# Attention layer of a hybrid backbone: rotated heads turned one block later, modulation vectors spread as two exact parts

## The chip, the cores and the metric

The kernel runs on one core of one Trainium2 chip. The time is the device time of one execution in microseconds, as the median of several runs. The engines are named as in the profile: PE (TensorE matmul; PEld its weight loads), DVE (VectorE), ACT (ScalarE), POOL (GpSimd) and SP (the queue that issues most of the DMAs).

## What is computed

Two layers over 256 latent tokens and 256 context tokens of width 1024. The first layer is attention, the second a state-space mixer; each is followed by a mixture of experts. The change lies in the first layer alone, up to its output projection. Cut to what matters:

```python
m  = split(silu(c) @ mod_w[layer] + mod_b[layer], 6)       # modulation of the latents
mc = split(silu(c_ctx) @ mod_w[layer] + mod_b[layer], 6)   # modulation of the context
xn = modulate(rms_norm(h, norm1_g), m[0], m[1])
hp = xn @ w_in                       # q and k of 8+2 heads, v, then q, k, v of 4 differential heads
qa, ka = rms_norm(qa, q_g), rms_norm(ka, k_g)
qa, ka, qb, kb = apply_rope(...)     # x * cos + rotated(x) * sin
p  = softmax(q @ k.T * scale)        # the differential heads: softmax(s1) - lam * softmax(s2)
h  = h + m[2] * (concat(p @ v) @ w_out)
h  = h + m[5] * hier_moe(modulate(rms_norm(h, norm2_g), m[3], m[4]))
```

A modulation vector is one row for all latent tokens and one for all context tokens. "Spreading" it means writing these two rows into all 128 partitions, 64 for each.

## The kernel before, in words

Latents and context are held together as four tiles of 128 rows (64 of the context, 64 latents). **Projection** (lines 474 to 572): the input weights come in five chunks (keys and values of the plain heads; their queries; queries of the differential heads; their keys; their values), and for each chunk there is a unit for each of the four row tiles. I call them blocks 0 to 19; block 4 is the first of the second chunk. Block `k` has a product `mm` and, if its chunk is rotated (blocks 0 to 15), a turn `tr`. `mm` is 8 x 3 matmuls into one PSUM bank (`mm3`, line 337: weights and activations are split in a high and a low part of type fp32r), then `rotate` (line 489), which is ACT's square (L495), a reduction, a reciprocal root in 12 tiny DVE operations (`rms`, line 282), a scaling (L500; these only in blocks 0 to 7) and the rotation itself (L505, L511 twice, L512), nearly all on DVE. `tr` (`head_pairs`, line 515) turns the rotated block on PE (L518), four transposes of 128 x 128 or one, and ACT copies it out (L530, L535 or L522).

The order is written out by hand with `pipeline` (line 189), which issues stage `n` of unit `k - lag[n]` in step `k`. With the lags (0, 2) the order on PE is mm(0), mm(1), mm(2), tr(0), mm(3), tr(1), mm(4), tr(2) and so on; the turn of a block waits for its L512.

The weights are split by `Splitter.half` (line 349): ACT rounds a quarter of a chunk to `whi` (L358), POOL computes `wlo` (L360). There are five buffers of each, so that of the next chunk only the first quarter is ready ahead; quarter 2 of a chunk takes the buffer that the last block of the chunk before gives up after its first six matmuls, and so on. Before block 12 the constants of the state-space layer are issued (`ssm_lambda`, line 1402): about a hundred small DVE operations, each in a fixed order behind the one before and behind block 11's rotation, and POOL copies of their results (L1508 to L1514).

**Attention** (lines 575 to 720): 48 head units (two query blocks, latents and context, four differential heads and eight plain ones each) with four stages at the lags (0, 3, 5, 10): scores and softmax, transposing the probabilities, the product with V, the last turn. Twelve more units are put in after every four or so of them, two for each of six modulation vectors (`mod_half`, line 229). Their first stage, `product`, is 8 matmuls of 1 MB of weights twice (L248) and an addition of the bias on DVE (L254) into the tile `mrow`; their second, `spread`, three units later, is one matmul of two rows picked by `sel2` (L258), and one copy or multiplication out of PSUM (L264, L266).

The compiler's scheduler sets each engine's final order by its own model from this order of issue; each engine then works its list in order. PSUM has six banks for all of this and two for the product with V. The tile pool `cx` holds eight score tiles `e`, two tiles `ob` and one `sq`.

```python
pipeline([unit(c, j) for c in range(5) for j in range(4)], (0, 2))          # line 572
t1 = (m5, H1[:, 0, :])[nrot[0] // 2 % 2][...]                               # line 503: four buffers
units.insert(10 * i + 5 * hf + 3, mod_half(*m[:3], hf, *m[3:]) + (None, None))  # line 718
pipeline(units, (0, 3, 5, 10))                                              # line 719
```

Of the kernel before, what the change touches and what calls it, by code (L numbers as in the profile page):

```python
# [10 lines left out]
F32 = mybir.dt.float32  # L11
# [3 lines left out]
FR = mybir.dt.float32r  # L15
AF = mybir.ActivationFunctionType
OP = mybir.AluOpType
# [113 lines left out]
def bc(ap, shape):  # L131
    return ap.to_broadcast(shape)
# [3 lines left out]
def hybrid(ctx: ExitStack, tc: tile.TileContext, A, out, taps=None, stop=None):  # L136
    nc = tc.nc
    taps = taps or {}
    V_ = nc.vector
# [29 lines left out]
    sm = ctx.enter_context(tc.tile_pool(name="sm", bufs=1))  # L169
# [3 lines left out]
    def bank(tag="b", name="bank"):  # L173
        return psp["p"].tile([128, 512], F32, tag=tag, bufs=psp[tag], name=name)
# [14 lines left out]
    def pipeline(units, lags):  # L189

        for k in range(len(units) + max(lags)):
            for n, lag in enumerate(lags):
                if 0 <= k - lag < len(units) and n < len(units[k - lag]) and units[k - lag][n]:
                    units[k - lag][n]()

    def wh(src, name, load=None):

        load = load or (lambda a: w8(a, name=name, shape=(4, 512)))
        hs = [load(src[:, 4 * i:4 * i + 4, :]) for i in range(2)]
        return lambda kk: hs[kk // 4][:, kk % 4, :]  # L200
# [8 lines left out]
    sel2 = cst[:, C_SEL2:C_SEL2 + 128]  # L209
# [16 lines left out]
    cp = [nc.scalar.copy, V_.tensor_copy]  # L226


    def mod_half(o, layer, sec, hf, sel, g=None, lean=False, room=None):


        n = 2 * sec + hf
        st = {}

        def product():
            w = wh(A["modw"][layer, n], "wmod", room and room[0])
            br = room[1] if room else brow
            sh = (lambda x: x) if len(br.shape) == 2 else (lambda x: x.rearrange("p (a b) -> p a b", b=128))
            nc.sync.dma_start(br[0:2], A["modb"][layer:layer + 1, n * 512:(n + 1) * 512].to_broadcast([2, 512])
                              if len(br.shape) == 2 else  # L240
                              sh(A["modb"][layer:layer + 1, n * 512:(n + 1) * 512]).to_broadcast([2, 4, 128]))
            if g is not None:
                st["gb"] = room[3] if room else sm.tile([128, 512], F32, tag="gb", bufs=1, name="gb")
                nc.sync.dma_start(st["gb"], g[:, hf * 512:(hf + 1) * 512].to_broadcast([128, 512]))
            pm = bank(name="pm")
            for kk in range(8):
                i = kk % 4
                nc.tensor.matmul(pm[32 * i:32 * i + 32, :], lhsT=cs[:, kk, :], rhs=w(kk), start=kk < 4, stop=kk >= 4)  # L248
            st["m"] = room[2] if room and room[2] is not None else sm.tile([128, 512], F32, tag="mrow", bufs=1, name="mrow")
            st["br"] = br  # L250
            if lean:
                nc.scalar.copy(st["m"], pm)
            else:
                V_.tensor_add(sh(st["m"]), sh(pm), br)  # L254

        def spread():
            pb = bank(name="pb")
            nc.tensor.matmul(pb, lhsT=sel, rhs=st["m"], start=True, stop=not lean)  # L258
            if lean:
                nc.tensor.matmul(pb if len(st["br"].shape) == 2 else pb.rearrange("p (a b) -> p a b", b=128), lhsT=sel,  # L260
                                 rhs=st["br"], start=False, stop=True)
            t = st["m"] if o is None else o[:, hf * 512:(hf + 1) * 512]
            if g is None:
                nc.scalar.copy(t, pb)  # L264
            else:
                V_.scalar_tensor_tensor(t, in0=pb, scalar=1.0, in1=st["gb"], op0=OP.add, op1=OP.mult)  # L266
            if o is None:
                for i in range(2):
                    nc.scalar.dma_start(md1[sec, i:i + 1, hf * 512:hf * 512 + 512], t[64 * i:64 * i + 1, :])
        return product, spread  # L270


# [99 lines left out]
    def attention(moe_mods, disp_open):  # L372
# [5 lines left out]
        def xo_pair():  # L378
            return [xo.tile([128, 8, 512], FR, tag=f"xo{i}", bufs=1, name="xo") for i in range(2)]
# [32 lines left out]
        units = []  # L412
# [129 lines left out]
        def unit(c, j):  # L542
# [26 lines left out]
                if nh:  # L569
                    head_pairs(st["t"], nh // 2, dst(j))  # L570
            return mm, tr
        pipeline([unit(c, j) for c in range(5) for j in range(4)], (0, 2))
        px.close()

        cx = actx.enter_context(tc.tile_pool(name="cx", bufs=1))
        OH, OL = xo_pair()
        m2 = H1[:, 0, :]

        def softmax_e(sp_, n):

            nm = sm.tile([128, 1], F32, tag="nm", bufs=6, name="nm")
            V_.tensor_reduce(nm, sp_[:, :n], axis=AX.X, op=OP.max, negate=True)  # L582
            e = cx.tile([128, 512], F32, tag="e", bufs=8, name="e")
            z = sm.tile([128, 1], F32, tag="z", bufs=6, name="z")
            nc.scalar.activation(e[:, :n], sp_[:, :n], AF.Exp, bias=nm, scale=1.0, accum_out=z)  # L585
            rz = sm.tile([128, 1], F32, tag="rzs", bufs=6, name="rz1")
            V_.reciprocal(rz, z)
            return e, rz
# [71 lines left out]
        def diff(b, lat):  # L660
            sh = {}
            nj, Vx = (4, V) if lat else (2, VC)

            def head(dh):
                st = {}

                def sc():
                    es, rzs = [], []
                    for i in range(2):
                        sp_, n = scores(qBT, dh, i, kBT[:, dh, :], b, lat)  # L670
                        e, rz = softmax_e(sp_, n)
                        es.append(e)
                        rzs.append(rz)
                    nl = sm.tile([128, 1], F32, tag="nl", bufs=4, name="nl")
                    V_.tensor_mul(nl, rzs[1], lam)
                    V_.tensor_scalar(es[1][:, :n], es[1][:, :n], nl, None, op0=OP.mult)
                    V_.scalar_tensor_tensor(es[0][:, :n], in0=es[0][:, :n], scalar=rzs[0], in1=es[1][:, :n],
                                            op0=OP.mult, op1=OP.subtract)
                    st["e"] = es[0]

                def tr():
                    st["P"] = cx.tile([128, 4, 128], F32, tag="P1", bufs=3, name="P1")
                    pT(st["e"], lat, st["P"])

                def pv():
                    if dh == 0:
                        sh["po"] = bank("po", name="po")
                    po = sh["po"]
                    for j in range(nj):
                        nc.tensor.matmul(po[:, dh * 128:(dh + 1) * 128], lhsT=st["P"][:, j],  # L690
                                         rhs=Vx[:, j, 128 + dh * 128:256 + dh * 128], start=j == 0, stop=j == nj - 1)
                    if dh < 3:
                        return
                    sq = cx.tile([128, 512], F32, tag="sq", bufs=1, name="sq")
                    nc.scalar.activation(sq, po, AF.Square)
                    ss = sm.tile([128, 4], F32, tag="oss", bufs=2, name="oss")
                    V_.tensor_reduce(ss, sq.rearrange("p (h d) -> p h d", h=4), axis=AX.X, op=OP.add)
                    r = rms(ss, 4, 128, "or")
                    ob = cx.tile([128, 4, 128], F32, tag="ob", bufs=2, name="ob")
                    V_.tensor_mul(ob, po.rearrange("p (h d) -> p h d", h=4), bc(r[:, :, None], [128, 4, 128]))  # L700
                    V_.tensor_mul(ob, ob, bc(sg[:, None, :], [128, 4, 128]))
                    sh["ob"] = ob

                def fin():
                    pt = bank(name="pt")
                    for i in range(4):
                        nc.tensor.transpose(pt[:, i * 128:(i + 1) * 128], sh["ob"][:, i, :], ident)
                    put_o(pt, 4, b, lat)
                return sc, tr, pv, fin if dh == 3 else None
            return [head(dh) for dh in range(4)]  # L710

        units = []
# [2 lines left out]
                units += diff(b, lat) + gqa(b, lat)  # L715
        for i, m in enumerate([(m2, 0, 2, sel2)] + moe_mods):
            for hf in range(2):
                units.insert(10 * i + 5 * hf + 3, mod_half(*m[:3], hf, *m[3:]) + (None, None))
        pipeline(units, (0, 3, 5, 10))
        actx.close()  # L720
        setup, squares, *steps = disp_open()
# [797 lines left out]
    S_ = {}  # L1519
# [585 lines left out]
```

## Time and profile before

| | |
|---|---|
| median of 3 runs | 1183.16 us (1179.98 to 1186.79) |
| the profiled execution | 1182.01 us, of which the span of the profile is 1180.2 us |
| mean granted TensorE clock | 0.881 of full speed |
| PE busy | 913.9 us (77%) |
| DVE busy | 625.1 us (53%) |
| ACT busy | 350.4 us (30%) |
| POOL busy | 270.7 us (23%) |

Stages, in microseconds from the span's start: the first modulation and the normalisation to about 58, the projection from 58 to 191, attention from 191 to 316, the output projection to 355, the routing to 405, the first mixture of experts to 590, the state-space layer to 850, the second mixture to the end.

The profile gives, for an instruction, when it began and how long it took; in brackets, how long its engine had been idle before it and what ended that. Matmuls are pipelined: one of 0.40 us may be followed by the next 0.23 us after its start, so the distance of starts is what a matmul costs in a row. fp32 matmuls appear as two instructions.

### The profile page before, as it was taken

How to read it: one execution, taken by the hardware profiler on the slowest of the kernel's cores; microseconds unless marked ns; L12 is line 12 of the kernel's file. 1: busy time of each engine (PE TensorE's matmuls, PEld its weight loads, DVE VectorE, ACT ScalarE, POOL GpSimd, SP SyncE). 2: the span in 40 equal slices, each digit the busy share in tenths (PEclk: the TensorE clock that was granted, in tenths of full speed). 3: DMA queues.
4: the chain of work that ended last, by engine and by line, in shares of the span. 5: the costliest groups of instructions: out<-in, count | busy, mean ns of one | idle time of the engine just before them, and what ended most of it. 6: DMA issues, size and time to landing. Idle time of an engine off the chain costs nothing. (4 is left out here: it accounts for less than half of the span.)

```text
span 1180.2 us, 15033 instructions
## 1 busy us (share of the span) xinstructions
PE 913.9 (77%) x5398; PEld 477.3 (40%) x5398; DVE 625.1 (53%) x1649; ACT 350.4 (30%) x705; POOL 270.7 (23%) x347
## 2 busy tenths in 40 slices
PE   3577989999898599787897896965289597776663
PEld 0365866434487333232332245712078441121110
DVE  1778794677549516553530038988847841111113
ACT  2332224756533212111120113713754320000001
POOL 0533321322422423132126305000045300000001
PEclk9798999999999599898898997986589797788797
DMA  9782222665653699998899974382356689999994
GB/s 289 269 217 71 72 72 72 215 230 201 233 224 137 226 377 408 415 372 332 345 415 344 406 268 122 144 335 107 141 175 257 249 324 420 420 420 420 420 420 166
DMA packets 54814, 317.14 MB, mean 269 GB/s; under 512 B 8587, under 2 KB 9627, under 8 KB 21712
## 3 DMA queue, kind: packets, MB, share of 16 engines
q1 hardware_dynamic: 42910, 285.49, 63.6%
q0 software_dynamic: 10080, 26.92, 6.2%
q10 hardware_dynamic: 1746, 3.73, 0.9%
q8 instruction: 44, 0.72, 0.2%
q14 instruction: 34, 0.28, 0.1%
HBM read 305.80 MB, written 19.94 MB: 276 GB/s over the span
## 5 line engine op out<-in xcount | busy, mean ns | idle before, releaser
L1251 PE MATMUL ph<-w,xgT 128*64 128x512 f32 x512 | 140.9, 629 | 10.0 <-DMA w<-in_gu 10.0
L248 PE MATMUL pm<-wmod,cs 128*32 128x512 f32 x352 | 52.0, 683 | 60.0 <-DMA wmod<-in_modw 51.8
L339 PE MATMUL pp<-wlo,xo 128*128 128x512 f32 (+1 forms) x224 | 88.5, 395 | 5.2 <-POOL wlo L360 5.0
L338 PE MATMUL pp<-whi,xo 128*128 128x512 f32 (+1 forms) x224 | 90.0, 402 | 1.3 <-ACT whi L358 1.3
L340 PE MATMUL pp<-whi,xo 128*128 128x512 f32 (+1 forms) x224 | 87.7, 392 | 0.0
L1277 PE MATMUL py<-w,hT 128*64 128x512 f32 x224 | 76.7, 646 | 0.9 <-DMA w<-in_dn 0.8
L1251 PEld LDWEIGHTS ph<-w,xgT 128*64 128x64 f32 x512 | 38.8, 141 | 78.2 <-issue 57.8
L360 POOL TENSOR_TENSOR wlo<-win,whi 128x1024 fp32r<-128x1024 f32 (+1 forms) x20 | 44.9, 2272 | 79.5 <-ACT whi L358 79.5
L1251 PE MATMUL ph<-w,xn 128*32 128x512 f32 x256 | 43.7, 771 | 23.7 <-DMA w<-in_gu 23.6
L1260 DVE TENSOR_TENSOR a<-a,ph 128x256 f32<-128x256 f32 x8 | 3.4, 422 | 101.1 <-ACT a L1259 101.1
L339 PEld LDWEIGHTS pp<-wlo,xo 128*128 128x128 f32 x224 | 44.6, 199 | 15.6 <-POOL wlo L360 7.8
L1260 DVE TENSOR_TENSOR hd<-sg,ph 128x256 f32<-128x256 f32 x16 | 6.7, 418 | 81.4 <-ACT sg L1259 81.4
L1303 PE MATMUL py<-w,m 128*32 128x512 f32 x256 | 42.5, 747 | 9.3 <-DMA w<-in_dn 8.7
L582 DVE TENSOR_REDUCE nm<-sc 128x1 f32<-128x512 f32 (+1 forms) x64 | 35.1, 551 | 26.2 <-PE sc L615 15.7
L338 PEld LDWEIGHTS pp<-whi,xo 128*128 128x128 f32 x224 | 44.8, 200 | 10.2 <-ACT whi L358 2.2
L340 PEld LDWEIGHTS pp<-whi,xo 128*128 128x128 f32 x224 | 44.4, 198 | 8.6
L248 PEld LDWEIGHTS pm<-wmod,cs 128*32 128x32 f32 x352 | 9.4, 115 | 88.6 <-issue 48.0
L1251 PE MATMUL ph<-w,xg 128*32 128x512 f32 x256 | 32.9, 640 | 14.4 <-DMA w<-in_gu 13.1
L363 POOL TENSOR_TENSOR wlo<-glu,whi 128x512 fp32r<-128x512 f32 x16 | 26.7, 1698 | 69.4 <-ACT whi L358 67.1
L1003 DVE SCALAR_TENSOR_TENSOR Yl<-py,WS,Yh 128x512 fp32r<-128x512 f32 x18 | 13.4, 750 | 54.5 <-ACT Yh L1002 41.9
L585 ACT ACTIVATE e<-sc,nm 128x512 f32<-128x512 f32 (+1 forms) x64 | 37.4, 586 | 12.7 <-DVE nm L582 8.4
L1277 PEld LDWEIGHTS py<-w,hT 128*64 128x64 f32 x224 | 22.1, 146 | 43.5 <-issue 40.4
(492 smaller groups left out, 1953.7 us busy)
## 6 DMA issues: line engine op xcount, KB each, us to landing
w<-in_gu SPq DMA_DIRECT2D x127, 1024.0 KB
w<-in_dn SPq DMA_DIRECT2D x62, 1024.0 KB
wmod<-in_modw SPq DMA_DIRECT2D x42, 1024.0 KB
win<-in_win SPq DMA_DIRECT2D x8, 1024.0 KB
glu<-in_glu SPq DMA_DIRECT2D x8, 1024.0 KB
yd<-in_zero SPq DMA_DIRECT2D x1, 4096.0 KB
wo<-in_wout SPq DMA_DIRECT2D x4, 1024.0 KB
w<-yd SPq DMA_DIRECT2D x4, 1024.0 KB
```

Of the source, the lines that this page charges most:

```text
L248: nc.tensor.matmul(pm[32 * i:32 * i + 32, :], lhsT=cs[:, kk, :], rhs=w(kk), start=kk < 4, stop=kk >= 4)
L338: nc.tensor.matmul(o, lhsT=lh, rhs=rh, start=start, stop=False)
L339: nc.tensor.matmul(o, lhsT=lh, rhs=rl, start=False, stop=False)
L340: nc.tensor.matmul(o, lhsT=ll, rhs=rh, start=False, stop=stop)
L360: self.engines[i].tensor_tensor(lw, w[:, 2 * i:2 * i + 2, :], hi.bitcast(F32), op=OP.subtract)
L363: e.tensor_tensor(lw[:, k], w[:, 2 * i + k, :], hi.bitcast(F32)[:, k], op=OP.subtract)
L582: V_.tensor_reduce(nm, sp_[:, :n], axis=AX.X, op=OP.max, negate=True)
L585: nc.scalar.activation(e[:, :n], sp_[:, :n], AF.Exp, bias=nm, scale=1.0, accum_out=z)
L1003: V_.scalar_tensor_tensor(Yl[:, s], in0=py, scalar=ws, in1=Yh[:, s].bitcast(F32), op0=OP.mult, op1=OP.subtract)
L1251: nc.tensor.matmul(ph[s, :], lhsT=st["x"][:, 4 * q + kk, s], rhs=g[:, i, kk % 2] if M.dma else g[:, i], start=(q, kk) == (0, 0), stop=(q, ...
L1277: nc.tensor.matmul(py[s, :], lhsT=st["hT"][:, fk, s], rhs=d[i][:, fk, hf * 512:hf * 512 + 512], start=fk == 0, stop=fk == 1)
L1303: nc.tensor.matmul(py[s, :], lhsT=st["hT"][:, fk, s], rhs=r, start=fk == 0, stop=fk == 1)
```

## The change

The projection's turns lag three blocks instead of two. For the twelve `mod_half` units of attention, the vector `m` is split into a rounded part of type fp32r (on ACT) and the exact rest (on DVE), and `spread` is two fp32r matmuls of these parts with a rounded copy of the selector (its elements are 0 and 1) instead of one fp32 matmul. The score tiles go from eight to seven, `ob` from two to one, and `sq` uses the tile of `row_ss`'s squares. Other uses of `mod_half` have no `parts` and stay as they are.

```diff
-    def mod_half(o, layer, sec, hf, sel, g=None, lean=False, room=None):
+    def mod_half(o, layer, sec, hf, sel, g=None, lean=False, room=None, parts=None):
...
                 V_.tensor_add(sh(st["m"]), sh(pm), br)
+            if parts:
+                st["p"] = [parts.tile([128, 512], FR, tag=n, bufs=1, name=n) for n in ("mh", "ml")]
+                nc.scalar.copy(st["p"][0], st["m"])
+                V_.tensor_tensor(st["p"][1], st["m"], st["p"][0].bitcast(F32), op=OP.subtract)

         def spread():
+            selr = S_.get("selr")
             pb = bank(name="pb")
-            nc.tensor.matmul(pb, lhsT=sel, rhs=st["m"], start=True, stop=not lean)
+            if parts:
+                for i in range(2):
+                    nc.tensor.matmul(pb, lhsT=selr, rhs=st["p"][i], start=i == 0, stop=i == 1)
+            else:
+                nc.tensor.matmul(pb, lhsT=sel, rhs=st["m"], start=True, stop=not lean)
...
-        pipeline([unit(c, j) for c in range(5) for j in range(4)], (0, 2))
+        pipeline([unit(c, j) for c in range(5) for j in range(4)], (0, 3))
         px.close()

         cx = actx.enter_context(tc.tile_pool(name="cx", bufs=1))
+        selr = cx.tile([128, 128], FR, name="selr")
+        V_.tensor_copy(selr, sel2)
+        S_["selr"] = selr
...
-            e = cx.tile([128, 512], F32, tag="e", bufs=8, name="e")
+            e = cx.tile([128, 512], F32, tag="e", bufs=7, name="e")
...
-                    sq = cx.tile([128, 512], F32, tag="sq", bufs=1, name="sq")
+                    sq = sm.tile([128, 512], F32, tag="junk", bufs=1, name="sq")
...
-                    ob = cx.tile([128, 4, 128], F32, tag="ob", bufs=2, name="ob")
+                    ob = cx.tile([128, 4, 128], F32, tag="ob", bufs=1, name="ob")
...
-                units.insert(10 * i + 5 * hf + 3, mod_half(*m[:3], hf, *m[3:]) + (None, None))
+                units.insert(10 * i + 5 * hf + 3, mod_half(*m[:3], hf, *m[3:], parts=cx) + (None, None))
```

## Rows read from the trace of the kernel before

**Rows 1.** The page's chain of work that ended last, shares by engine.

```profile
DMA 17%; PE 1%; DVE 1%; ACT 0%; issue 0%; POOL 0%; SPq 0%; POOLq 0%; ACTq 0%
```

**Rows 2.** Busy time by stretch: PE, PEld, DVE, ACT, POOL, then clock, DMA share, GB/s.

```profile
61.80:124.30 62.50, 48.97 (x226) 39.88 (x225) 54.37 (x154) 18.41 (x41) 18.89 (x8) 0.89 0.45 124
...
190.90:316.20 125.30, 119.40 (x649) 56.98 (x648) 88.58 (x280) 82.76 (x250) 34.59 (x64) 0.99 0.60 209
...
405.00:590.00 185.00, 160.25 (x880) 62.04 (x882) 85.24 (x176) 36.06 (x70) 47.37 (x61) 0.93 0.95 374
```

**Rows 3.** Whom PE waited for in the projection: total, times, longest.

```profile
PE pt L518 <- DVE m L512: 9.5, 3, 4.7
PE pt L518 <- DVE H L512: 4.1, 2, 2.3
PE pp L339 <- POOL wlo L360: 4.0, 2, 3.8
```

**Rows 4.** Timeline of PE in the projection: start, duration.

```profile
83.54 0.48 PE L338 MATMUL pp<-whi,xo 128*128 128x512 f32 x1
...
89.22 0.27 PE L518 MATMUL pt<-cst,H 128*128 128x128 f32 x1
...
106.33 1.09 PE L518 MATMUL pt<-cst,m 128*128 128x128 f32 x4 [4.74 <-DVE m L512]
...
117.63 0.48 PE L338 MATMUL pp<-whi,xo 128*128 128x512 f32 x1
...
124.86 0.60 PE L518 MATMUL pt<-cst,H 128*128 128x128 f32 x4
...
131.25 0.48 PE L338 MATMUL pp<-whi,xo 128*128 128x512 f32 x1
```

**Rows 5.** Timeline of DVE in the projection.

```profile
61.88 0.29 DVE L497 TENSOR_REDUCE hs<-b 128x2 f32<-128x128 f32 x1 [3.88 <-ACT b L495]
...
98.69 2.34 DVE L309 SCALAR_TENSOR_TENSOR rz<-rz,rt 128x8 f32<-128x8 f32 x1
...
119.83 0.17 DVE L309 SCALAR_TENSOR_TENSOR rz<-rz,rt 128x8 f32<-128x8 f32 x1
...
123.56 0.69 DVE L512 TENSOR_TENSOR H<-H,b 128x512 f32<-128x512 f32 x1
```

**Rows 6.** Timeline of ACT and of POOL in the projection.

```profile
106.28 0.60 ACT L495 ACTIVATE b<-pp 128x512 f32<-128x512 f32 x1 [6.36 <-DVE m L512]
106.78 1.98 ACT L358 CAST whi<-win 128x1024 fp32r<-128x1024 f32 x2
...
107.89 4.73 POOL L360 TENSOR_TENSOR wlo<-win,whi 128x1024 fp32r<-128x1024 f32 x2 [4.57 <-ACT whi L358]
...
166.16 4.68 POOL L360 TENSOR_TENSOR wlo<-win,whi 128x1024 fp32r<-128x1024 f32 x2
...
179.68 0.29 POOL L1511 COPY LR<-H 64x128 f32<-64x128 f32 x1
```

**Rows 7.** Timeline of PE around one spread in attention.

```profile
203.04 0.47 PE L602 MATMUL sc<-kAH,qs 128*128 128x512 f32 x1
203.45 0.50 PE L603 MATMUL sc<-kAL,qs 64*128 64x512 f32 x1
203.88 1.13 PE L258 MATMUL pb<-mrow,cst 128*128 128x512 f32 x2
204.44 0.79 PE L602 MATMUL sc<-kAH,qs 128*128 128x512 f32 x1
205.16 0.50 PE L603 MATMUL sc<-kAL,qs 64*128 64x512 f32 x1
```

**Rows 8.** Groups of instructions in attention: busy, mean ns, idle before.

```profile
L254 DVE TENSOR_TENSOR mrow<-pm,brow 128x512 f32<-128x512 f32 x12 | 8.2, 686 | 4.8 <-PE pm L248 4.8
...
L264 ACT COPY H<-pb 128x512 f32<-128x512 f32 x2 | 1.2, 586 | 0.7 <-PE pb L258 0.7
```

**Rows 9.** Whom PE waited for in attention, one of six lines.

```profile
PE sc L602 <- POOL qs L597: 1.2, 1, 1.2
```

## The prediction

> **What bounds the kernel now.** I read the chain of waits first: it is followed back only into the second mixture of experts and stands there on weight DMAs [rows 1], so it says nothing of the first layer. Next came busy time by stage [rows 2]. In the first mixture (405 to 590) the DMA engines are busy for 0.95 of the time; that stage begins when the routing before it is done, and no row shows it waiting for a point of time of its own. So a microsecond taken out of projection or attention should arrive at the end.
>
> In the projection PE is the engine that the rest follows, and it waits 13.6 us for L512, the last step of a rotation, at five turns, and 4.0 us for split weights [rows 3]. The reader should see in the first row of [rows 2] that from 61.8 to 124.3 DVE is busy 54.4 of 62.5 us: the rotations of blocks 0 to 7 run one after the other without a real pause, from 61.88 to 123.56 + 0.69 = 124.25 [rows 5]. They are slow partly because of POOL: a DVE step on 8 numbers takes 0.17 us alone and 2.34 us while POOL splits weights [rows 5]. So there are two limits in this stretch: DVE's list, and PE standing at turns whose rotation isn't ready.
>
> In attention PE is busy 119.4 of 125.3 us, DVE 88.6, ACT 82.8 [rows 2]: PE bounds it, with 5.9 us of idle time.
>
> **The lag.** Today mm(11) starts at 131.25 [rows 4]: the turn of block 7 goes out at 124.86, behind mm(9), and mm(10) comes after it. With a lag of three that turn stands behind mm(10), so mm(10) is done while DVE still rotates. Two limits for the new start of mm(11):
> - DVE: its list doesn't get shorter. Block 7's rotation ends at 124.25, its turn takes 0.35 us (from 124.86 to the product after it), so mm(11) starts at 124.65 at the earliest. The gain is at most 131.25 - 124.65 = 6.6 us.
> - PE: mm(8) needs the last quarter of its weights. ACT casts it behind block 6's square, which ends at 106.88 because it waits for block 5's rotation; POOL then takes 4.73 / 2 = 2.4 us from 107.89 [rows 6]. So that quarter is there at 110.25, and PE will wait for it where it now waits for a turn. Six matmuls remain. A block of 24 in a row takes from 83.54 to 89.22, 5.7 us or 0.237 each [rows 4]; after a wait it takes 7.2 us (117.63 to 124.86), because the granted clock is then low for the first of them (0.89 in the mean of this stretch [rows 2]). At full clock mm(8) ends at 111.7, and mm(9) and mm(10) with their turns end at 124: DVE's limit decides. At the lower clock mm(8) ends at about 112.8, mm(9) takes 7.2, mm(10) 5.7, the turns 0.7, and mm(11) starts at 126.4: a gain of 4.8.
>
> I take the middle of 4.8 and 6.6, **5.7 us**. What is late next is DVE. Behind mm(11) all follows from mm(11): the next quarters' buffers, block 11's rotation and, fixed behind it, the constants of the state-space layer and POOL's copies. The 3.8 us that PE waits for the last chunk's weights [rows 3] hang on those copies, so they move and stay. Of the moved turns, the transposes are the same in number and ACT's copies out of PSUM follow them; no DMA moves. The four buffers of rotated blocks suffice: block k needs the buffer of block k - 4, whose turn stands behind mm(k - 1).
>
> **The spread.** L602 and L603 follow each other at 0.41 to 0.43 us. From the spread at 203.88 to the L603 at 205.16 are 1.28 us, which hold the spread and one such step: the spread costs 0.86 [rows 7]. Its replacement is two one-pass products of full height; 24 of these with a fresh weight load each take 0.237 [rows 4], so 0.47 for the pair. The other bound is the step of 0.42 of L602 and L603, which are one-pass products too, with the load not hidden: 0.84 for the pair. I take 0.47, since these are of full height like the projection's. PE then saves 12 x 0.39 = 4.7 us, at least 12 x 0.02 = 0.2.
>
> Added are twelve copies on ACT at 0.59 and twelve subtractions on DVE at 0.69 [rows 8], 7 and 8.3 us. They raise ACT to 90 and DVE to 97 of 125 us: neither becomes the bound by its sum. The chain is covered: a spread comes three units behind its product, about 3 x 125.3 / 60 = 6.3 us, and addition, copy and subtraction take 2.0 us. If a subtraction is late, the spread waits on PE with the next head's scores queued behind it; if the cover failed each time, the price would be 12 x 1.28 = 15.4 us. More work in two queues that softmax uses also makes PE's waits longer: with load up by 9% on both I let the 5.9 us grow by a third, 2 us. Net **2.7 us**, between -10.7 (all uncovered) and +4.7.
>
> **The rest.** The selector's copy is one small DVE operation ahead of attention. Seven score tiles: a differential unit takes two and gives one back within the unit, so with a lag of three about six are held; I cost this at nothing, and if the cover is gone ACT's exponential waits for a transposition which is next on PE's list. `ob` is written every twelve units or more and read five later: one suffices. `sq` is used by ACT in order either way.
>
> **Sum.** 5.7 + 2.7 = 8.4 us against the profiled execution's 1182.01 gives 1173.6; that execution is 1.15 under the median of 1183.16, which would give 1174.8. I say 1174.
>
> **Rivals.**
> - *Weights take the turns' place.* The scheduler sets ACT's order. If the other two casts of the second chunk also come to stand behind block 6's square, three splits follow 107.89 and end at 115.0; mm(8) ends at 116.4, mm(11) starts at 116.4 + 3 x 0.35 + 2 x 5.7 = 128.9, and the lag gives 2.4 instead of 5.7. Time: 1177.5. For it: one of three casts stands there already [rows 6]. Against: nothing in the edit moves that square.
> - *The subtractions cost more than the products save.* A subtraction reads two SBUF tiles, as L309 does, which took 2.34 instead of 0.17 beside POOL [rows 5]; POOL holds scores here, and PE has waited for it once [rows 9]. If each subtraction holds POOL's next step back by its 0.69 us and PE with it, 12 x 0.69 = 8.3 us stand against 4.7: the change gives 5.7 - 3.6 = 2.1, time 1181. Against: POOL is busy only 34.6 of 125.3 us here [rows 2], so fewer than a third should meet. [...]
> - *The new products aren't cheap* (the change doesn't do what it says): 0.84 for the pair saves nothing, the waits of 2 us stay, and 5.7 - 1.8 = 3.9 is left: 1179.
> - *Slower: the last chunk's splits fall behind POOL's copies.* Two of them stand at 166.16, between copies; the last copy ends at 179.97 [rows 6]. If the scheduler puts them behind it, they end at 184.65 instead of 170.84, 13.8 us later, and block 16 waits that long. Less 8.4 this is 5.4 us slower than before, 1188.5; with the gains at their low ends up to 1194. It decides from the point where the splits come behind more than the pair of copies that are ahead of them now. For it: that wait exists. Against: rotation and constants keep their order.
> - *Better:* those splits come ahead of all copies, the 3.8 us go, 1170.
>
> **Numbers.** Forecast 0.48, weights 0.16, subtractions 0.14, products 0.10, slower 0.07, better 0.05. A measurement of this kernel tells some 0.5% (5.9 us) from no change: below 1177.2 is faster, above 1189.1 slower. The forecast and the better case lie below, of the weights' case about half, of the products' case and the slower case a part: faster 0.63, same 0.30, slower 0.07. The range from 1168 to 1182 holds all but the slower case and the edges of the others.
>
> **What would show it.** Right: PE's waits at L518 for L512 fall from 13.6 us to below 4; a new wait of PE for L360 or L358 of some 4 to 6 us near 104 to 110; mm(11) starts near 125.5; block 7's L512 still ends near 124; the distance over a spread falls from 1.28 to about 0.9 us; attention lasts some 122.5 us; routing and both mixtures keep their lengths. Wrong: PE's waits for L512 unchanged in sum, mm(11) at 129 or later, attention longer than 125.3 us, or a wait for L360 at block 16 well over 3.8 us.

## The result, and the profile after

The changed kernel is **slower** by 0.9 per cent: 1192.42 us in the median of 11 runs (1185.61 to 1198.21) against 1183.16 (1177.31 to 1186.79) for the kernel before, a ratio of 1.0087 with a 95% interval of 1.0063 to 1.0111: small, but clear of the noise. Its profiled execution took 1193.16 us with a span of 1191.3, against 1180.2. Its lines stand 9 lower in the file than before in the projection and 12 lower in attention (L518 is now L527, L602 is L614); the new copy is L257, the new subtraction L258, the spread L265.

| stage, us | before | after |
|---|---|---|
| start to the first score of attention | 190.9 | 186.4 |
| attention (to the out-projection's first product) | 126.6 | 136.8 |
| from there to the first product of L864 (now L876), routing | 40.4 | 42.1 |
| from there to the end | 822.2 | 826.0 |

The first score came 4.5 us earlier. Attention gave back 10.2. Each row is of one execution: in all fourteen kernels of this document the first score lies at 190.4, 190.9 and 193.1 us with the lag of two and between 186.4 and 188.8 with the lag of three, so the lag's gain is clear, but its size is known only to some two microseconds. The last row is not read as an effect: in the twelve runs below, whose code is the same there, it lies between 814 and 835.

Whom PE waited for in the projection, after (to be set beside [rows 3]):

```profile
PE pp L348 <- POOL wlo L369: 10.7, 7, 3.8
PE pt L527 <- DVE H L521: 1.9, 1, 1.9
PE pp L347 <- ACT whi L367: 1.0, 2, 0.5
```

The waits for rotations fell from 13.6 to 1.9 us, and waits for split weights took their place. In the timeline of PE (beside [rows 4]) three of these stand in mm(8), at 104.00, 106.52 and 109.04; the turn of block 7 is now behind mm(10), and mm(11) starts at 126.43 instead of 131.25, 4.8 earlier:

```profile
104.00 0.50 PE L348 MATMUL pp<-wlo,xo 128*128 128x512 f32 x1 [2.30 <-POOL wlo L369]
...
109.04 0.50 PE L348 MATMUL pp<-wlo,xo 128*128 128x512 f32 x1 [0.85 <-POOL wlo L369]
...
118.46 0.63 PE L527 MATMUL pt<-cst,H 128*128 128x128 f32 x4 [1.95 <-DVE H L521]
...
126.08 0.60 PE L527 MATMUL pt<-cst,H 128*128 128x128 f32 x4
126.43 0.48 PE L347 MATMUL pp<-whi,xo 128*128 128x512 f32 x1
```

In attention the spread is as cheap as was said. In the timeline of PE (beside [rows 7]) the first one-pass product starts at 199.56 and the second score product behind it at 200.45, 0.89 us where it was 1.28:

```profile
199.13 0.49 PE L615 MATMUL sc<-kAL,qs 64*128 64x512 f32 x1
199.56 0.50 PE L265 MATMUL pb<-mh,selr 128*128 128x512 f32 x1
199.89 0.39 PE L265 MATMUL pb<-ml,selr 128*128 128x512 f32 x1
200.12 0.40 PE L614 MATMUL sc<-kAH,qs 128*128 128x512 f32 x1
200.45 0.49 PE L615 MATMUL sc<-kAL,qs 64*128 64x512 f32 x1
```

And yet attention is longer. Its row of busy time by stretch (columns as in [rows 2]), and whom PE waited for in it (beside [rows 9]):

```profile
186.40:323.20 136.80, 123.84 (x649) 59.52 (x648) 97.03 (x296) 89.10 (x265) 33.55 (x64) 0.93 0.54 191
```

```profile
PE sc L614 <- POOL qs L609: 6.3, 4, 3.4
PE pb L265 <- ACT mh L257: 1.8, 2, 1.1
PE pt L634 <- ACT e L597: 1.6, 1, 1.6
PE pt L634 <- ACT mh L257: 1.1, 1, 1.1
```

Two things are to be seen. PE now waits 6.3 us, not 1.2, for the low part of the query (`qs`). And PE is busy for 123.84 us although its work got shorter: the granted clock is 0.93 in this stage, where it was 0.99 [rows 2]. The clock's record has one stretch at half clock (0.5 of full speed) in attention before, of 3.4 us, and four after, of 3.4, 3.4, 6.8 and 6.8.

### The profile page after: what moved, and what is told of

Same layout as the page of the kernel before. It is cut to its first block, busy times and chain, and to the rows that moved or that the text cites. A ratio compares the mean times of both kernels' runs of the same rounds, so it can differ in the third digit from the quotient of the medians.

```text
span 1191.3 us, 15051 instructions
## 1 busy us (share of the span) xinstructions
PE 912.5 (77%) x5398; PEld 477.0 (40%) x5398; DVE 635.1 (53%) x1662; ACT 354.6 (30%) x717; POOL 270.8 (23%) x347
## 5 line engine op out<-in xcount | busy, mean ns | idle before, releaser
L248 PE MATMUL pm<-wmod,cs 128*32 128x512 f32 x352 | 56.8, 721 | 63.1 <-DMA wmod<-in_modw 55.0
L348 PE MATMUL pp<-wlo,xo 128*128 128x512 f32 (+1 forms) x224 | 89.1, 398 | 11.8 <-POOL wlo L369 11.7
```

The lines of the kernel that those rows point to most:

```text
L348: nc.tensor.matmul(o, lhsT=lh, rhs=rl, start=False, stop=False)
```

## The experiments

Theory A at the start: the twelve copies and subtractions crowd ACT's and DVE's queues. All times by stage are of one profiled execution each; the ratio is that of the timed runs to those of the kernel before on the same chip. "Idle" is the time, up to attention's last matmul, in which no matmul ran (each kernel has 1.3 us more of it between that one and the out-projection's first); "half clock" is what the clock's record shows within attention.

| kernel | first score | attention | idle | half clock | ratio [95%] |
|---|---|---|---|---|---|
| before | 190.9 | 126.6 | 5.9 | 3.4 | 1 |
| after | 186.4 | 136.8 | 11.7 | 20.5 | 1.0087 [1.0063, 1.0111] |
| lag3_only | 186.6 | 126.6 | 5.9 | 3.4 | 0.9961 [0.9934, 0.9989] |
| parts_only | 190.4 | 134.6 | 11.6 | 13.7 | 1.0070 [1.0042, 1.0097] |
| memory_only | 193.1 | 126.6 | 5.9 | 3.4 | 1.0018 [0.9988, 1.0048] |
| copy_on_pool | 187.7 | 133.4 | 13.5 | 6.8 | 1.0095 [1.0057, 1.0133] |
| load_only | 187.5 | 130.0 | 8.9 | 3.4 | 1.0013 [0.9973, 1.0052] |
| high_only | 187.1 | 128.8 | 10.7 | 10.2 | 0.9979 [0.9948, 1.0011] |
| split_later | 187.0 | 133.0 | 9.7 | 13.7 | 0.9999 [0.9966, 1.0031] |
| copy_on_dve | 187.5 | 135.9 | 11.6 | 13.7 | 1.0024 [0.9992, 1.0056] |
| old_order | 186.4 | 128.4 | 10.3 | 3.4 | 0.9985 [0.9957, 1.0013] |
| high_only_old_order | 187.4 | 123.7 | 8.4 | 3.4 | 0.9875 [0.9814, 0.9937] |
| load_only_old_order | 187.4 | 128.3 | 8.4 | 0 | 1.0000 [0.9971, 1.0029] |
| old_order_pool | 188.8 | 128.9 | 9.2 | 6.8 | 1.0015 [0.9987, 1.0043] |

**Which part of the change.** Three kernels each make one part of it.

```diff
# lag3_only: the kernel before with
-        pipeline([unit(c, j) for c in range(5) for j in range(4)], (0, 2))
+        pipeline([unit(c, j) for c in range(5) for j in range(4)], (0, 3))
# parts_only: the changed kernel with (0, 2) there
# memory_only: the kernel before with
-            e = cx.tile([128, 512], F32, tag="e", bufs=8, name="e")
+            e = cx.tile([128, 512], F32, tag="e", bufs=7, name="e")
-                    sq = cx.tile([128, 512], F32, tag="sq", bufs=1, name="sq")
+                    sq = sm.tile([128, 512], F32, tag="junk", bufs=1, name="sq")
-                    ob = cx.tile([128, 4, 128], F32, tag="ob", bufs=2, name="ob")
+                    ob = cx.tile([128, 4, 128], F32, tag="ob", bufs=1, name="ob")
```

> Only the rotated heads are turned three blocks behind; old spread, old buffers. Theory A (the new copy and subtraction of the vectors crowd ACT's and DVE's queues during attention): the first score comes at about 186.4 us as in the changed kernel, attention (first score to first out-projection product) stays at 126.6 us give or take 2, time about 1178.5 us, ratio 0.996. Rival (the earlier end of the projection shifts attention against its weight loads, so the lag itself lengthens it): first score 186.4, attention 133 us or more, time 1186 us or more.

> The changed kernel with the heads turned two blocks behind again: the split vectors and the buffers that were cut for them are left. Theory A: first score at 190.9 us, attention 135 to 138 us against 126.6, time 1192 to 1198 us, ratio about 1.011. Rival (lag): attention about 125 us, time 1180 to 1183 us.

> The kernel before with only the smaller buffers: seven tiles of exponentials for eight, one tile of normed heads for two, the squares in the shared scratch tile. Theory A: attention 126.6 us give or take 1.5, time 1183 us (ratio 0.999 to 1.002). Rival M (the cut buffers make the waits): attention 133 us or more, time 1189 us or more.

Theory A's numbers came for the lag and the buffers; for the split vectors the side came, the size just missed (134.6 us for 135 to 138, a ratio of 1.0070 for 1.011). The lag alone leaves attention at 126.6 us to a tenth, with the same waits, and is faster, 0.9961. The smaller buffers alone do nothing (126.6). The split vectors alone make attention 134.6 us, with the very 6.3 us of waits for `qs`. So the loss lies in the split vectors; the lag is not its cause.

This pair also tells how far one execution can be trusted. In attention parts_only has the order of the changed kernel on all four engines, and the same idle time (11.6 and 11.7 us), yet it took 134.6 us and not 136.8: one stretch of half clock fewer. So a difference of some 2 us between two rows of the column "attention" can be the clock's, unless their stretches of half clock are the same.

**Where it waits.** The longest wait, on PE in the changed kernel, and ahead of it POOL and ACT:

```profile
278.31 0.80 PE L614 MATMUL sc<-kAH,qs 128*128 128x512 f32 x1 [3.37 <-POOL qs L609]
```

```profile
277.00 0.71 POOL L656 TENSOR_SCALAR e<-e,rz 128x512 f32<-128x512 f32 x1 [0.98 <-DVE rz L599]
277.80 0.87 POOL L609 TENSOR_TENSOR qs<-qAT,qs 64x128 fp32r<-64x128 f32 x2
```

```profile
273.18 0.60 ACT L707 ACTIVATE sq<-po 128x512 f32<-128x512 f32 x1
273.77 0.69 ACT L597 ACTIVATE e<-sc,nm 128x512 f32<-128x512 f32 x1
274.36 0.19 ACT L597 ACTIVATION_READ_ACCUMULATOR e<-sc,nm 128x1 f32 x1
274.45 0.57 ACT L635 COPY P<-pt 128x512 f32<-128x512 f32 x1
275.01 0.59 ACT L273 COPY mrow<-pb 128x512 f32<-128x512 f32 x1
275.50 0.69 ACT L597 ACTIVATE e<-sc,nm 128x512 f32<-128x512 f32 x1
276.08 0.20 ACT L597 ACTIVATION_READ_ACCUMULATOR e<-sc,nm 128x1 f32 x1
276.31 0.49 ACT L608 CAST qs<-qAT 64x128 fp32r<-64x128 f32 x2
```

ACT has no pause from 273.18 on. The cast of the query, a third of a microsecond long and needing nothing new, stands behind two exponentials and two copies; POOL's low part comes behind a normalisation that waits for the second of these. The same place in ACT's timeline with the lag alone:

```profile
270.73 0.59 ACT L695 ACTIVATE sq<-po 128x512 f32<-128x512 f32 x1
271.35 0.29 ACT L596 CAST qs<-qAT 64x128 fp32r<-64x128 f32 x1
271.67 0.59 ACT L623 COPY P<-pt 128x512 f32<-128x512 f32 x1
272.28 0.69 ACT L585 ACTIVATE e<-sc,nm 128x512 f32<-128x512 f32 x1
272.86 0.19 ACT L585 ACTIVATION_READ_ACCUMULATOR e<-sc,nm 128x1 f32 x1
273.08 0.30 ACT L596 CAST qs<-qAT 64x128 fp32r<-64x128 f32 x1
273.40 0.59 ACT L264 COPY mrow<-pb 128x512 f32<-128x512 f32 x1
```

Here one cast stands right behind the square and the next behind the exponential: **the order in the queue is another one**. In the four kernels below that are held to an order, ACT worked its queue in that order: all 253 of its old instructions of attention run so. The order is laid down when the kernel is built, by the scheduler (the planner of the expectations), and it is not the program's. The lag alone leaves every engine's instructions of attention in the order of the kernel before. In the changed kernel at most 222 of ACT's 253, 241 of DVE's 283 and 55 of POOL's 64 still stand in it.

**Which engine, which side.** Before the order was suspected, five kernels asked whether one engine is crowded, and whether the added work or the shorter products open the waits.

```diff
# copy_on_pool (copy_on_dve: V_.tensor_copy)
-                nc.scalar.copy(st["p"][0], st["m"])
+                nc.gpsimd.tensor_copy(st["p"][0], st["m"])
# load_only: parts made, but spread as before
-            if parts:
-                for i in range(2):
-                    nc.tensor.matmul(pb, lhsT=selr, rhs=st["p"][i], start=i == 0, stop=i == 1)
-            else:
-                nc.tensor.matmul(pb, lhsT=sel, rhs=st["m"], start=True, stop=not lean)
+            nc.tensor.matmul(pb, lhsT=sel, rhs=st["m"], start=True, stop=not lean)
# high_only: no copy, no subtraction, one product (cut to the addition)
...
+                V_.tensor_add(sh(st["p"][0]), sh(pm), br)
...
# split_later: copy and subtraction as a stage of their own
+        def parting():
...
-        return product, spread
+        return (product, parting, spread) if parts else (product, spread)
-        pipeline(units, (0, 3, 5, 10))
+        pipeline([u if len(u) == 5 else (u[0], None) + u[1:] for u in units], (0, 1, 3, 5, 10))
```

> The changed kernel with the copy that makes the high part on POOL in place of ACT. Theory A in its narrow form (ACT's in-order queue, the copy ahead of the query casts): attention falls from 136.8 to 131 us or less, time 1187 us or less, ratio to before 1.003 or less. Rival Q (POOL is itself in the chain, through the query's low part and the normalising products, and its copy is longer): attention 137 us or more, time 1192 us or more. Rival M: no change, 1192 us.

> The changed kernel with the copy to the high part on DVE in place of ACT. If ACT alone is crowded: attention 131 us or less, time 1186 us or less. If DVE is as crowded (it also holds the row maxima and reciprocals on which the exponentials and POOL wait): attention 136 us or more, time 1191 us or more.

> The changed kernel, lag of three, with the copy and the subtraction still made, but the vectors spread by the old single fp32 product from the unsplit row; the two parts are used by nothing. Theory A (the 24 added instructions on ACT and DVE make the waits, and the waits let TensorE's clock fall): TensorE still waits 4 us or more in all for the query's low part, more than one stretch of half clock, attention 133 us or more, time 1184 us or more. Rival F (the old product covered the other engines' work, and taking it away is what opens the waits): attention 126.6 to 129 us, one stretch of half clock as in the kernel before, time 1177 to 1180 us.

> The low part is left out: DVE's bias addition writes the rounded high part itself, and one one-pass product spreads it; no copy, no subtraction. TensorE's work falls by about 12 x 0.8 us against the old spread with nothing added elsewhere. Theory A: attention 118 to 123 us, time 1168 to 1174 us. Rival F: the products were not what bounds attention; it stays at 126 us or more, with new waits or half-clock stretches, time 1177 us or more.

> The changed kernel with the copy and the subtraction issued one block after the product, in a stage of their own; the same instructions. If the place in ACT's queue is what costs (the copy ahead of the query casts): attention 131 us or less, time 1186 us or less. If the number of instructions is what costs: attention 135 us or more, time 1190 us or more.

No one theory fits all five. On POOL the copy leaves 133.4 us, with new waits (6.0 us for the normed heads), and the run is no faster; on DVE it leaves 135.9. The load by itself costs 130.0 - 126.6 = 3.4 us, between the two forecasts. The shorter products by themselves, with nothing added anywhere, do not shorten attention: 128.8 us against 126.6 with the lag alone, with 6.8 us more at half clock, and ratios whose intervals overlap. Theory A had 118 to 123 and was wrong; rival F's numbers came. One block later the same instructions cost 3.8 us less, between the two forecasts. In each of the five the scheduler had laid ACT's queue anew (at most 218 to 231 of the 253 stand in the old order), so that none of them separates load from order.

**The order.** These kernels hold every engine's old instructions in attention to the order of the kernel with the lag alone (for each engine a list of ranks, and a bond from each instruction to the one ahead of it); the new ones go in between.

```diff
...
+        for en, ranks in ORDER.items():
+            mine = [i for i in done if str(i.engine) == "EngineType." + en and i.name not in free]
+            for r, s in zip(ranks, ranks[1:]):
+                tc.add_manual_dep(mine[s], mine[r].name, mybir.DependencyInfo(
+                    mybir.DependencyClass.NoSync, mybir.DependencyReason.DATA), reason="order")
...
```

> The changed kernel with its instructions, lag and buffers, but in attention every engine's old instructions are held to the order that they have in the kernel with the lag alone; only the copies, the subtractions and the second products stand in between. Theory O (the planner, given shorter products and more copies, orders ACT's and DVE's queues anew, with query casts behind exponentials, and that order makes the waits): attention 127 us or less, at most one stretch of half clock more, time 1178 us or less. Theory L (the added instructions themselves, in whatever order): attention 133 us or more, three or four stretches of half clock, time 1187 us or more.

> The high part alone (low part left out, no copy, no subtraction), in the order of the kernel with the lag alone. Theory O: the shorter products now show, attention 118 to 123 us against 128.8 in the planner's order. Rival F (attention has other chains of the same length as TensorE's): 125 us or more, with waits that grow by what the products lose.

> Copy and subtraction made and unused, the old fp32 spread, in the order of the kernel with the lag alone. Theory O: attention 126 to 128 us, since both hide beside the old product. Theory L: 130 us as in the planner's order.

Attention by stretch, with the lag alone, then in old_order, then in high_only_old_order:

```profile
186.60:313.20 126.60, 119.45 (x649) 56.99 (x648) 88.94 (x283) 84.01 (x253) 34.48 (x64) 0.99 0.59 207
```

```profile
186.40:314.80 128.40, 116.78 (x650) 57.76 (x649) 95.91 (x296) 90.25 (x266) 35.06 (x64) 0.99 0.59 204
```

```profile
187.40:311.10 123.70, 113.98 (x638) 55.84 (x637) 89.22 (x284) 83.72 (x254) 33.98 (x64) 0.99 0.60 212
```

With the same instructions, buffers and lag, the old order takes attention from 136.8 to 128.4 us: **8.4 of the 10.2 us are the order**, by one execution of each and so to some 2 us; the timed runs stand as far apart (0.9985 and 1.0087, with intervals that do not meet). The clock is back at 0.99, and that is most of it: idle time fell by 1.3 us, the time in which matmuls ran by 7.1 (123.84 to 116.78). Theory O named 127 or less, so it was not the whole: 1.8 us against the lag alone remain, at the same 3.4 us of half clock. The load is a likely cause, not a shown one: with the old spread the copies and subtractions cost 128.3 - 126.6 = 1.7 in the old order (just outside theory O's 126 to 128), though without a stretch of half clock. The shorter products of high_only_old_order do pay, 126.6 - 123.7 = 2.9 us, between the two forecasts and not the 12 x 0.8 = 9.6 that theory A had expected of them: the time in which matmuls ran fell by 5.5 (119.45 to 113.98), and idle time grew by 2.6. Two waits of old_order that the lag alone has shorter (0.8 and 1.2):

```profile
PE pt L730 <- DVE ob L724: 2.4, 2, 2.0
PE sc L625 <- POOL qs L620: 2.2, 2, 1.7
```

**A last try.** The copy and the subtraction both on POOL, in the old order, to take the load off ACT and DVE.

```diff
-                free.add(nc.scalar.copy(st["p"][0], st["m"]).ins.name)
-                free.add(V_.tensor_tensor(st["p"][1], st["m"], st["p"][0].bitcast(F32), op=OP.subtract).ins.name)
+                free.add(nc.gpsimd.tensor_copy(st["p"][0], st["m"]).ins.name)
+                free.add(nc.gpsimd.tensor_tensor(st["p"][1], st["m"], st["p"][0].bitcast(F32), op=OP.subtract).ins.name)
```

> The changed kernel held to the order of the kernel with the lag alone, with both the copy and the subtraction on POOL, which is busy a quarter of attention. If what is left of the cost in that order is the load on ACT and DVE: attention 124 to 126.5 us, time 1173 to 1177 us, below the lag alone. If POOL's queue is itself in the chain (the query's low part and the normalising products stand behind the copies): attention 129 us or more, time 1180 us or more.

128.9 us, ratio 1.0015: the rival's side, a tenth short of its 129. POOL's groups in that stretch show why; a subtraction takes 1285 ns there, and PE waited for it 1.3 us in two spreads:

```profile
L268 POOL TENSOR_TENSOR ml<-mrow,mh 128x512 fp32r<-128x512 f32 x12 | 15.4, 1285 | 0.8
```

No version with the exact split beat the lag alone. The fastest kernel, high_only_old_order, leaves the low part out and so computes less.

## Why the prediction was wrong

- **The lag: right, at its lower end or just under it.** Of the two limits PE's decided: mm(11) at 126.43, where the text had 126.4 for a clock that stays low after a wait. The middle of 4.8 and 6.6 was taken, 4.5 came at the first score. The slowing is in the trace: after the wait at 118.46 the products come at 0.43 us for some 3 us. Block 7's rotation ended at 125.00, not 124.25. The wait for mm(8)'s last quarter came, in three pieces. Of the rivals on this part neither happened: no cast slipped as far as mm(11) at 128.9, and the longest wait for the last chunk is still 3.8 us.
- **The products: right in the row, too large in the sum.** At the row that was read a spread is 0.39 us shorter, as worked out (0.89 against 1.28). Over all of attention the time in which matmuls ran fell by 2.7 us in old_order against the lag alone (119.45 to 116.78), not by 12 x 0.39 = 4.7.
- **The subtractions beside POOL: one meeting in twelve.** Eleven subtractions ran while POOL did nothing and took 679 to 693 ns. The one at 307.22 met POOL and took 875, and POOL's low part of the query that began inside it took 763, against a median of 454; PE waited 0.56 us for that low part. So what the rival supposed came once and smaller: POOL's step took 0.31 us longer, and in none of the twelve was one held back by a whole subtraction (0.69 us). The text was right that the two would seldom meet.

```profile
L258 DVE TENSOR_TENSOR ml<-mrow,mh x12: 679/688/875, 195.6 to 318.8; 128x512 fp32r<-128x512 f32 x12
L609 POOL TENSOR_TENSOR qs<-qAT,qs x32: 449/454/763, 188.1 to 308.4; 64x128 fp32r<-64x128 f32 x32
```

```profile
306.50 1.06 POOL L656 TENSOR_SCALAR e<-e,rz 128x256 f32<-128x256 f32 x2 [1.55 <-DVE rz L599]
307.22 0.88 DVE L258 TENSOR_TENSOR ml<-mrow,mh 128x512 fp32r<-128x512 f32 x1
307.64 1.18 POOL L609 TENSOR_TENSOR qs<-qAT,qs 64x128 fp32r<-64x128 f32 x2
```

- **The step that failed** is in "The spread": "More work in two queues that softmax uses also makes PE's waits longer: with load up by 9% on both I let the 5.9 us grow by a third, 2 us." The idle time grew by 5.8, and the price of a wait was taken as the wait alone. What the sentence left out is that the edit changes the order in which the old instructions stand in the queues (8.4 us), and that stretches of half clock follow some waits, in which a product takes nearly twice as long (0.43 us for 0.23). With the order held, 2.7 us of products gained stand against 4.5 of idle time, a loss of 1.8 instead of the net gain of 2.7 (4.7 less 2); as built, the loss is 10.2. The lower bound of the text was -10.7, for a subtraction that is late each time: nearly the size, but by luck, since the mechanism was another: the waits of PE that the profile puts down to `mh` were only 2.9 us of it. No rival had this case; the one slower rival put its loss in the projection.
- **The total.** -4.5 at the first score, +10.2 in attention, +1.7 between attention and routing, and 3.8 behind that which the spread of the runs covers: 11.1 in the profiled spans, 9.3 in the medians. The sum forecast was -8.4.
- The buffers, and that the stages behind move with attention's end, were as said.

What stays open: which engine's order does the harm (all four were held at once), and why the scheduler lays it so; only that it did is shown. The converse, the new order with the old instructions, was not run. How the waits of that order lead to the stretches of half clock is argued from where they stand, not shown.

## What to carry to other kernels

Where a scheduler lays the queues, an edit has two prices, that of its instructions and that of the order in which all others come to stand; compare each engine's sequence before and after, above all the short casts that feed the next product, and hold the old order in a second kernel to tell the two apart. Taking work off an engine that is busy for 94% of a stage (PE, 119.45 of 126.6 us) paid only in part: 2.9 us of 5.5, as its idle time grew by 2.6. A wait of PE cost more than its length where the clock fell with it (0.51 from 276.3 to 283.2 in the changed kernel, around the end of the wait of 3.37 us at 278.31), so count the granted clock of the stage along with the waits.

## What the runs showed of the hardware

Small waits were followed by long slow stretches, but not always. In the changed kernel PE stood for 0.74, 1.67, 3.37 and 1.11 us within 4 us of the four falls of the clock to its lower level (0.50 or 0.51 of full speed), and each fall held for 3.4 or 6.8 us. A wait of the same kind, 0.73 us, stands in parts_only at 212.28 with no fall behind it, and in all fourteen kernels PE waits 1.6 and 0.7 us in the first ten microseconds of attention and no fall follows. The sum of idle time does not tell it either: copy_on_pool idled 13.5 us and had 6.8 us at half clock, the changed kernel 11.7 and 20.5.

The clock also fell behind next to no wait. In the out-projection of the changed kernel the products' step goes from 0.23 to 0.43 us at 341.2, and the last time that PE stood before was for 0.24 us at 338.0:

```profile
340.84 0.40 PE L349 MATMUL pp<-whi,xo 128*128 128x512 f32 x1
341.08 0.52 PE L347 MATMUL pp<-whi,xo 128*128 128x512 f32 x1
341.40 0.63 PE L348 MATMUL pp<-wlo,xo 128*128 128x512 f32 x1
341.82 0.63 PE L349 MATMUL pp<-whi,xo 128*128 128x512 f32 x1
...
344.73 0.40 PE L347 MATMUL pp<-whi,xo 128*128 128x512 f32 x1
```

That is the 1.7 us of the table's third row. It comes in six of the fourteen profiled executions (the changed kernel, parts_only, high_only, old_order, load_only_old_order and old_order_pool) and not in the other eight, though all fourteen have the same wait of 0.24 us at that place; no run here says why.
